# Delta-rule and HGRN2 weights split behind the ended stage's evictions, low parts on VectorE

## The chip, the cores and the metric

One core of a Trainium2 chip. The metric is device time in microseconds. The number shown as before is the median of 3 runs; one further execution was recorded by the hardware profiler, and all rows below are of that execution.

## The reference

One inference step over two layers of a hybrid decoder. Each layer normalizes the stream, multiplies it by one wide input projection, gives groups of columns to four mixers (A = HGRN2, B = gated delta rule, C = Mamba-2 SSD, D = retention), gates their outputs and multiplies them by an output projection. Each mixer reads 2048 prompt tokens, 16 meta tokens ahead of them, and 8 sample tokens that continue stored states.

```python
def layer(h):                       # cut from the reference, in outline
    u = rms_norm(h, w) @ W_in       # columns for A | B (qkv, gate, beta, a) | C (xBC, z, dt) | D
    yA = hgrn2(u_A)                 # vector decay, chunked
    yB = gated_delta(causal_conv(u_B))   # serial over chunks
    yC = ssd(causal_conv(u_C))
    yD = retention(rotary(u_D))
    return h + W_out @ concat(gate * y)
```

## The kernel before

The prompt and the samples lie in 17 tiles: tile 0 with 40 rows (16 meta and 8 sample tokens, padded), and 16 chunks of 128 tokens. Dense work goes over 8 blocks of two tiles (block 0 has three tiles and 296 columns, the others 256). Every layer runs its mixers as stages, in this order: C, B, A, D, output projection. B's dense work comes first in its stage; its serial part, the walk over chunks (`walkB`), is issued in pieces between the work of A and D.

A dense product is made exact enough by splitting both factors into a high and a low part (x = xh + xl, w = wh + wl): three matmuls for each of eight slices of the inner dimension, L484 to L486 in `dense_cm` (weights as the stationary operand, columns of tokens moving), into a tile `pd`; there are two such tiles. A piece of 128 output columns is 24 matmuls for a block; B has eight such pieces (six for q, k, v, which go through a causal convolution, and two for the gate z).

Weights come in pieces of 128 x 1024 numbers (`wpiece`): a transfer into a raw tile `wr` from a pool of five buffers, issued on SP (L451); a cast to the high part `wh` on ScalarE (L458); and a subtraction `wl = wr - wh` (L459), on GpSimd or on VectorE. Which of these two engines it is comes from `lopool`: 1 puts all on GpSimd, 0 all on VectorE, 2 alternates. The stage sets it from the constants PC0, PC1, PB, PA, PD, PO before it calls `weightsB` and so on.

The program is written stage by stage; a scheduler turns it into a queue for each engine, and an engine runs its queue in order. `early()` raises the priority of what is issued under it, so that the scheduler takes it as soon as its inputs are there: the weights of the next stage are split while the stage before still runs. `inorder(names)`, an existing helper, finds the last instruction that has been issued on each named engine, and keeps what is issued under it behind these.

What the names in the rows are: `pd` is a dense product; `u`, `bqk`, `bv` are B's pieces before and after the convolution (L944 to L946 copy them out, L956 and L958 are the taps, L962 and L963 the activation), `cx`, `cb`, `cc` are C's (L954, L958, L962, L963); `z` is a gate (L532, L533). In stage C the chunk work of a tile goes from scores (`tr<-cc,cb`) to a masked product `css` on GpSimd (L1453), a weighted input `cxw` (L1467), the state `SC` (L1479), the output `coi` (L1492 to L1496), a group norm (`fsq`, `fm`, `on`: L606, L612, L616) and a last multiplication on ScalarE into `y` (L1510). The eight samples of tile 0 go through their own steps in between (`decode`) and end with the 40-column `y`, which needs a transfer of the row `dcr` (L1559) first.

Of the kernel before, what the change touches and what calls it, by code (L numbers as in the profile page):

```python
# [93 lines left out]
def body(tc, ctx, a, o, nch, depth, blks, off):  # L94
# [45 lines left out]
    def flush():  # L140
        while pend:
            pend.pop(0)()
# [3 lines left out]
    def hook(n=1):  # L146

        credit[0] += n
        while credit[0] >= 1:
            credit[0] -= 1  # L150
            if walk and next(walk[0], 0) == 0:
                walk.pop()

    @contextmanager
    def inorder(names):

        seen, left = {}, set(names)
        for i in reversed(nc.cur_bb.bb.instructions):
            e = i.engine
            if e in left:  # L160
                seen[e] = i
                left.discard(e)
                if not left:
                    break
        with ExitStack() as st:
            for i in seen.values():
                st.enter_context(tc.issue_after(i))
            yield
# [10 lines left out]
    rA, rB, rD = 1, 1, 1  # L179
    DVEI = ()  # L180
    lopool = [0, 0]
    PC0, PC1, PB, PA, PD, PO = 1, 1, 1, 2, 0, 0
    ACOPY = 1
    WD = 0
    GQ = 1
# [3 lines left out]
    ET = mybir.EngineType  # L189
# [4 lines left out]
    def early():  # L194
        return tc.high_priority(offset=3000)
# [26 lines left out]
    def f4(shape, name, dt=F32):  # L222
        return fp.tile(shape, dt, tag="f4", name=name)
# [38 lines left out]
    def fill():  # L262
        nc.sync.dma_start(cst, a["c_tab"])
        tri = w1([128, 128], "tri")
        nc.sync.dma_start(tri, a["c_retm"][:, 704:832])
        V.tensor_copy(l128r, tri)
        V.tensor_scalar(nbf, C("u32c"), -NEG, NEG, ALU.mult, ALU.add)
        V.tensor_copy(ibf, ident)
        tt(strict, C("u32c"), C("hm0"), ALU.subtract)
        for x in (*sbd, tb, wz, hones):  # L270
            G.memset(x, 0.0)
        G.memset(hones[0:64, 0:1], 1.0)
        G.memset(hones[64:128, 1:2], 1.0)
# [191 lines left out]
    def load_tm(w, cols, wide=False):  # L465
        n = sum(c[1] for c in cols)
        nd = 2 if n == 512 else 4
        r = 128 * nd
        return [wpiece([w[r * k:r * k + r, c0:c0 + cn] for c0, cn in cols], nd, n, wide and k < 2) for k in range(8 // nd)]
# [4 lines left out]
    def load_x(b):  # L474
        b.xh, b.xl = xpair(b.i % 2, BW if b.i % 2 == 0 else 256)
        nc.sync.dma_start(f32(b.xh[:, :, 0:b.n]), f32(xhd[b.i][:, :, :]))
        nc.sync.dma_start(f32(b.xl[:, :, 0:b.n]), f32(xld[b.i][:, :, :]))
# [231 lines left out]
    def weightsA(w):  # L709
        return ([load_cm(w, A_Q + 128 * p) for p in range(2)], [load_cm(w, A_F + 128 * p) for p in range(2)],  # L710
                load_tm(w, [(A_I, 256)]), [load_cm(w, A_Z + 128 * p, True) for p in range(2)])
# [300 lines left out]
    def weightsB(w):  # L1012
        return [load_cm(w, B_QKV + 128 * i) for i in range(6)], [load_cm(w, B_Z + 128 * p, True) for p in range(2)]

    def denseB(L, W, b):

        b.qk, b.v = [blk("bqk") for _ in range(2)], blk("bv")
        qkv = [b.qk[p][:, x] for x in range(2) for p in range(2)] + [b.v[:, p] for p in range(2)]
        conv(L, W[0], b, 0, "B", False, qkv)
        z = blk("z")  # L1020
        for p in range(2):
            dense_cm(W[1][p], b, lambda ps: silu2(ps, z[:, p, 0:b.n], b.n))
            hook(rB)
        nc.sync.dma_start(zdr[b.i], z[:, :, 0:b.n])
        for dst, src in ((slice(0, 4, 2), b.qk[0]), (slice(1, 4, 2), b.qk[1]), (slice(4, 6), b.v)):
            for r in (slice(0, 32), slice(TR0, b.n)) if b.first else (slice(0, b.n),):
                nc.sync.dma_start(qkvd[b.i][:, dst, r], src[:, :, r])
        if b.last:
            conv_out(L, "B", o["gdn_conv_p"][L.l])
# [362 lines left out]
    def weightsC(w):  # L1392
        W = load_tm(w, [(C_Z, 256), (C_Z + 256, 4), (B_AB, 8)], True), []
        for i in range(6):
            if i % 2 == 0:
                yield W
            W[1].append(load_cm(w, C_XBC + 128 * i))
        yield W
# [302 lines left out]
    def prep0(L, b):  # L1701
        b.xh, b.xl = xpair(b.i % 2, BW if b.i % 2 == 0 else 256)
        for t in b.tiles:
            hx = f4([128, D], "hx")
            load_h(0, t, hx)
            xprep(L, t, hx, True)
        for dst, src in ((xhd, b.xh), (xld, b.xl)):
            nc.sync.dma_start(f32(dst[b.i][:, :, :]), f32(src[:, :, 0:b.n]))

    def decode(L, left=False):  # L1710

        while L.dec is not None:
            with inorder(ORD):
                if next(L.dec, 0) == 0:
                    L.dec = None
            if not left:
                return
# [4 lines left out]
    for l in range(depth):  # L1722
        L = Ln
        L.dec = None
        w = a["w_in"][l]
        nextx = (lambda b: prep0(L, b)) if l == 0 else load_x
        if l == 0:
            nextx(blocks[0])
            lopool[0] = PC0
            W = list(weightsC(w))[-1]  # L1730
            fill()
            next(ld)
        else:
            nextx(blocks[0])
        for b in blocks:
            if not b.last:
                nextx(blocks[b.i + 1])
            mixC(L, W, b)
            if not b.first:
                decode(L)  # L1740
        decode(L, True)
        lopool[0] = PB
        with early():
            W = weightsB(w)
        load_x(blocks[0])
        P = None
        walk.append(walkB(L))
        for i in range(-1, nblk, 2):
            bs = blocks[max(i, 0):i + 2]
            for b in bs:  # L1750
                if not b.last:
                    load_x(blocks[b.i + 1])
                denseB(L, W, b)
                if L.dec is not None:
                    decode(L)
            if P is not None:
                L.walkq.append(P)
                if P.first:
                    credit[0] = -WD
            if WEARLY and bs[-1].last:  # L1760
                lopool[0] = PA
                with early():
                    W = weightsA(w)
            with early():
                P = prepB(L, bs)
            if P.first:
                L.dec = decB(L, P.ys, P.epsq)
            decode(L)
        L.walkq.append(P)
        while L.dec is not None:  # L1770
            hook()
            decode(L)
        for x in sq128:
            G.memset(x, 0.0)
        for weights, mix in ((weightsA, mixA), (weightsD, mixD)):
            if not (WEARLY and weights is weightsA):
                lopool[0] = PD
                with early():
                    W = weights(w)
            load_x(blocks[0])  # L1780
            for b in blocks:
                if not b.last:
                    load_x(blocks[b.i + 1])
                mix(L, W, b)
                if not b.first:
                    decode(L)
            flush()
            decode(L, True)
        while walk:
            hook()  # L1790
        lopool[0] = PO
        with early():
            W = [load_tm(a["w_out"][l], [(512 * qd, 512)], qd == 0) for qd in range(2)]
        if l + 1 < depth:
            ld = load_layer(l + 1)
            Ln = next(ld)
            next(ld)
        else:
            Ln = None
            fnw = f4([128, D], "fnw")  # L1800
            nc.sync.dma_start(fnw, a["final_norm_w"].partition_broadcast(128))
        for t in range(NT):
            if t == NT - 1 and Ln is not None:
                lopool[0] = PC1
                parts = weightsC(a["w_in"][l + 1])
                W = outproj(L, W, t, Ln, parts)
            else:
                outproj(L, W, t, Ln)
# [48 lines left out]
```

## Time and profile before

| | |
|---|---|
| median of 3 runs | 2852.36 us (2849.44 to 2856.09) |
| profiled execution, its own time | 2860.07 us |
| its span, first to last instruction | 2858.1 us |
| mean granted TensorE clock | 0.978 of full speed |
| TensorE, matmuls | 2702.7 us, 95% of the span |
| VectorE | 1712.1 us, 60% |
| ScalarE | 1038.7 us, 36% |
| GpSimd | 1066.1 us, 37% |

An engine's busy time is the sum of its instructions in the recorded execution. The profiled execution was 7.7 us longer than the median of the others.

### The profile page before, as it was taken

How to read it: one execution, taken by the hardware profiler on the slowest of the kernel's cores; microseconds unless marked ns; L12 is line 12 of the kernel's file. 1: busy time of each engine (PE TensorE's matmuls, PEld its weight loads, DVE VectorE, ACT ScalarE, POOL GpSimd, SP SyncE). 2: the span in 40 equal slices, each digit the busy share in tenths (PEclk: the TensorE clock that was granted, in tenths of full speed). 3: DMA queues.
4: the chain of work that ended last, by engine and by line, in shares of the span. 5: the costliest groups of instructions: out<-in, count | busy, mean ns of one | idle time of the engine just before them, and what ended most of it. 6: DMA issues, size and time to landing. Idle time of an engine off the chain costs nothing.

```text
span 2858.1 us, 64542 instructions
## 1 busy us (share of the span) xinstructions
PE 2702.7 (95%) x25300; PEld 2461.8 (86%) x25300; DVE 1712.1 (60%) x4872; ACT 1038.7 (36%) x2621; POOL 1066.1 (37%) x2032
## 2 busy tenths in 40 slices
PE   6989999989999899999988999999999999999998
PEld 6889898889889789888878999989888887888887
DVE  5677765657656655464445767756676666445533
ACT  4445532333434422232243445223334443222321
POOL 4453546468323221210032535556673322212100
PEclk9999999999999999999999999999999999999999
DMA  7243455463321423236772423544632223331443
GB/s 177 69 139 106 148 136 146 130 175 103 108 74 61 149 77 113 77 99 212 224 227 80 127 104 115 154 121 140 181 106 72 76 89 109 99 102 67 145 140 111
DMA packets 385143, 349.16 MB, mean 122 GB/s; under 512 B 144312, under 2 KB 349616, under 8 KB 374600
## 3 DMA queue, kind: packets, MB, share of 16 engines
q1 hardware_dynamic: 381320, 335.95, 38.7%
q0 software_dynamic: 3520, 9.09, 1.6%
q8 instruction: 200, 3.28, 0.5%
q14 instruction: 103, 0.84, 0.1%
HBM read 247.05 MB, written 98.10 MB: 121 GB/s over the span
## 4 chain that ended last, share of the span: by engine, by line
PE 76%; DVE 8%; DMA 6%; ACT 3%; POOL 3%; issue 2%; SPq 1%; POOLq 0%; ACTq 0%; DVEq 0%
PE pd L494 10%; PE pd L495 9%; PE pd L497 9%; PE pd L484 9%; PE pd L485 9%; PE pd L486 9%; PE tr L236 7%; PE wo L236 4%; PE sc L236 4%; PE o L236 3%; DMA wr<-in_w_in_dram 3%; PE tr L623 1%; ACT wh L458 1%; PE tr L519 1%; DMA bld<-qkv 1%
## 5 line engine op out<-in xcount | busy, mean ns | idle before, releaser
L484 PE MATMUL pd<-xh,wh 128*128 128x256 f32 (+1 forms) x2816 | 826.9, 294 | 36.9 <-ACT wh L458 11.6
L485 PE MATMUL pd<-xl,wh 128*128 128x256 f32 (+1 forms) x2816 | 817.6, 290 | 0.0
L486 PE MATMUL pd<-xh,wl 128*128 128x256 f32 (+1 forms) x2816 | 813.2, 289 | 1.2 <-DVE wl L459 0.7
L484 PEld LDWEIGHTS pd<-xh,wh 128*128 128x128 f32 x2816 | 542.5, 193 | 58.1 <-issue 15.0
L494 PE MATMUL pd<-wh,xh 128*128 128x512 f32 (+5 forms) x1632 | 563.8, 346 | 8.1 <-DVE sraw L1409 5.1
L495 PE MATMUL pd<-wl,xh 128*128 128x512 f32 (+5 forms) x1632 | 560.0, 343 | 3.8 <-POOL wl L459 3.8
L485 PEld LDWEIGHTS pd<-xl,wh 128*128 128x128 f32 x2816 | 542.1, 193 | 5.5 <-issue 2.7
L486 PEld LDWEIGHTS pd<-xh,wl 128*128 128x128 f32 x2816 | 542.5, 193 | 4.5 <-issue 1.7
L497 PE MATMUL pd<-wh,xl 128*128 128x512 f32 (+4 forms) x1600 | 544.6, 340 | 0.0
L494 PEld LDWEIGHTS pd<-wh,xh 128*128 128x128 f32 (+1 forms) x1632 | 307.1, 188 | 44.8 <-issue 5.5
L495 PEld LDWEIGHTS pd<-wl,xh 128*128 128x128 f32 (+1 forms) x1632 | 307.4, 188 | 38.8 <-POOL wl L459 4.2
L497 PEld LDWEIGHTS pd<-wh,xl 128*128 128x128 f32 (+1 forms) x1600 | 299.8, 187 | 34.7 <-issue 2.0
L313 DVE TENSOR_TENSOR sbd<-low,tr 64x128 f32<-64x128 f32 x384 | 108.9, 284 | 122.0 <-PE tr L236 110.5
L336 POOL TENSOR_TENSOR fm<-fm,expo 128x4 f32<-128x4 f32 (+3 forms) x136 | 133.0, 978 | 85.4 <-DVE fm L614 78.0
L612 POOL TENSOR_SCALAR fm<-fm 128x4 f32<-128x4 f32 (+3 forms) x102 | 22.1, 216 | 363.2 <-DVE fm L609 335.8
L1683 DVE TENSOR_TENSOR hx<-hx,pd 128x512 f32<-128x512 f32 (+1 forms) x72 | 49.5, 687 | 153.1 <-PE pd L497 148.0
L340 POOL TENSOR_SCALAR rm<-rm 128x1 f32<-128x1 f32 (+1 forms) x51 | 14.1, 277 | 337.6 <-ACT junk L358 336.7
L244 POOL COPY bwi<-wz 32x256 f32<-32x256 f32 x128 | 58.7, 458 | 197.9 <-DVE wz L1267 195.6
L1171 POOL TENSOR_TENSOR bR<-bR,bW 128x120 f32<-128x120 f32 (+14 forms) x300 | 118.5, 395 | 20.3
L532 ACT ACTIVATE th<-pd 128x256 f32<-128x256 f32 (+2 forms) x162 | 62.6, 386 | 174.4 <-PE pd L486 130.3
L1170 POOL TENSOR_TENSOR bW<-bU,bR 128x120 f32<-128x120 f32 (+14 forms) x300 | 114.0, 380 | 29.8 <-DMA bR<-bscr 9.5
L458 ACT CAST wh<-wr 128x1024 fp32r<-128x1024 f32 x80 | 83.1, 1044 | 89.1 <-DMA wr<-in_w_in_dram 67.3
(524 smaller groups left out, 5055.7 us busy)
## 6 DMA issues: line engine op xcount, KB each, us to landing
xh<-xh SPq DMA_DIRECT2D x56, 1024.0 KB
xl<-xl SPq DMA_DIRECT2D x56, 1024.0 KB
wr<-in_w_in_dram SPq DMA_DIRECT2D x64, 512.0 KB
hx<-in_x_prompt_dram SPq DMA_DIRECT2D x32, 512.0 KB
y<-y SPq DMA_DIRECT2D x128, 128.0 KB
yf<-y SPq DMA_DIRECT2D x32, 512.0 KB
bld<-qkv SPq DMA_DIRECT2D x32, 384.0 KB
xh<-xh SPq DMA_DIRECT2D x8, 1184.0 KB
```

Source lines behind the costliest of these rows:

```text
L236: T.matmul(out, l, r, start=start, stop=stop, skip_group_check=True)
L313: tt(new[rr, :, hh], low[rr, :, hh], pv, ALU.add)
L336: G.tensor_tensor(dst, src, e.broadcast_to(list(src.shape)), ALU.pow)
L458: S.copy(hv[:, :, c0:c1], r)
L484: T.matmul(ps, hi[:, d], b.xh[:, d, 0:b.n], start=(d == 0), stop=False)
L485: T.matmul(ps, hi[:, d], b.xl[:, d, 0:b.n], start=False, stop=False)
L486: T.matmul(ps, lo[:, d], b.xh[:, d, 0:b.n], start=False, stop=(d == 7))
L494: T.matmul(ps[0:R, 0:n], xh[:, d], hi, start=(d == 0), stop=False)
L495: T.matmul(ps[0:R, 0:n], xh[:, d], lo, start=False, stop=xl is None and d == 7)
L497: T.matmul(ps[0:R, 0:n], xl[:, d], hi, start=False, stop=(d == 7))
L1170: f(wv, bcm(U_[0:2 * nu, j, j + 1:32], 1, m), bcl(R_[0:2 * nu, 0:m, j], 31 - j), ALU.mult)
L1171: f(R_[0:2 * nu, 0:m, j + 1:32], R_[0:2 * nu, 0:m, j + 1:32], wv, ALU.subtract)
```

## The change

Two constants are set to 0, so that the subtractions of B's and of A's weights all go to VectorE (before: B's all on GpSimd, A's alternating). And the two places that issue these weights stand under `inorder` for ScalarE and VectorE, so that the casts and subtractions come behind the last instruction that was issued there on each of the two engines. The weights of C, D and of the output are not touched.

```diff
-    PC0, PC1, PB, PA, PD, PO = 1, 1, 1, 2, 0, 0
+    PC0, PC1, PB, PA, PD, PO = 1, 1, 0, 0, 0, 0
...
         decode(L, True)
         lopool[0] = PB
-        with early():
+        with early(), inorder((ET.Activation, ET.DVE)):
             W = weightsB(w)
...
             if WEARLY and bs[-1].last:
                 lopool[0] = PA
-                with early():
+                with early(), inorder((ET.Activation, ET.DVE)):
                     W = weightsA(w)
```

How the queues change. On ScalarE, at the end of stage C in layer 0, the queue before has the casts of B's weights between C's last evictions (`cx`, `cb`, `cc`):

```order
L458 CAST wh<-wr 128x1024
L954 ACTIVATE cb<-pd,cbh,cwh 128x256
L962 ACTIVATE th<-cb 128x256
L458 CAST wh<-wr 128x1024 x2
L954 ACTIVATE cc<-pd,cbh,cwh 128x256
L977 COPY cso<-tr 3x384
L458 CAST wh<-wr 128x1024
L954 ACTIVATE cc<-pd,cbh,cwh 128x256
```

The queue of the changed kernel on ScalarE at the same place in the program, from C's last outputs on, down to the first copy of B's first piece:

```order
L1510 ACTIVATE y<-tr,pv 128x128 x2
L606 ACTIVATE fsq,fm<-coi 40x128 x2
L989 COPY cxt<-tr 128x3x24 x2
L1510 ACTIVATE y<-tr,pv 128x40 x2
L458 CAST wh<-wr 128x1024 x7
L944 COPY u<-pd 128x32
L945 COPY usB<-pd 128x8
L946 COPY u<-pd 128x256
L956 ACTIVATE bqk<-u,cwh 128x32
L458 CAST wh<-wr 128x1024
```

The casts have moved behind the output of the sample tile, and seven of the eight stand in a row ahead of the first copy of B's dense product.

On TensorE, before, the matmuls of B's block 0 (128x296) come directly behind C's last dense matmuls (128x256) and a few small ones:

```order
L485 MATMUL pd<-xl,wh 128x256
L486 MATMUL pd<-xh,wl 128x256
L976 MATMUL tr<-ident,hC 3x128
L236 MATMUL tr<-g,cst 128x8
L236 MATMUL tr<-g,l128r 128x8
L236 MATMUL tr<-g,cst 128x8 x2
L976 MATMUL tr<-ident,hC 3x128
L484 MATMUL pd<-xh,wh 128x296
L485 MATMUL pd<-xl,wh 128x296
```

In the changed kernel TensorE's queue has, ahead of B's block 0 in layer 0, the whole chunk work of C's last tiles and the transposes of its outputs (these rows are the end of it):

```order
L236 MATMUL wo<-cxb,css 128x64 x4
L236 MATMUL wo<-SC,cc 128x128 x2
L236 MATMUL tr<-cxw,cxb 128x128 x2
L623 MATMUL tr<-ident,on 128x128 x4
L623 MATMUL tr<-ident,on 128x40
L986 MATMUL tr<-ident,cx 128x96 x2
L623 MATMUL tr<-ident,on 128x40
L484 MATMUL pd<-xh,wh 128x296
L485 MATMUL pd<-xl,wh 128x296
L484 MATMUL pd<-xh,wh 128x296
L485 MATMUL pd<-xl,wh 128x296
L486 MATMUL pd<-xh,wl 128x296
```

B's dense matmuls have moved behind all of these, with no dense matmul between them any more.

On VectorE, at the end of B's dense work in layer 0, the queue before has a subtraction for A's weights between the taps of B's last convolution piece:

```order
L1267 TENSOR_TENSOR wz<-bwi,wo 32x256
L958 SCALAR_TENSOR_TENSOR bv<-pd,cwh,bv 128x256 x2
L459 TENSOR_TENSOR wl<-wr,wh 128x1024
L958 SCALAR_TENSOR_TENSOR bv<-pd,cwh,bv 128x256
L960 COPY hB<-pd 128x3
```

In the changed kernel, the same place on VectorE:

```order
L958 SCALAR_TENSOR_TENSOR bv<-pd,cwh,bv 128x256 x3
L960 COPY hB<-pd 128x3
L385 TENSOR_SCALAR cwh<-cwt 128x48
L963 SCALAR_TENSOR_TENSOR bv<-th,bv 128x256
L645 SCALAR_TENSOR_TENSOR y<-tr,pvh,bz 128x128 x2
L533 SCALAR_TENSOR_TENSOR z<-th,pd 128x256
L1267 TENSOR_TENSOR wz<-bwi,wo 32x256
L313 TENSOR_TENSOR sbd_112<-low,tr 64x2x64
L533 SCALAR_TENSOR_TENSOR z<-th,pd 128x256
L313 TENSOR_TENSOR sbd_112<-low,tr 64x2x64
L1267 TENSOR_TENSOR wz<-bwi,wo 32x256
L459 TENSOR_TENSOR wl<-wr,wh 128x1024 x2
```

The three taps, the closing step and both gate pieces of B's last block have moved ahead of the first subtraction for A; ScalarE's queue shows the same for its part.

## Rows read from the trace of the kernel before

**Rows 1.** The page: span; busy time, share of the span, instructions of TensorE.

```profile
span 2858.1 us, 64542 instructions
...
PE 2702.7 (95%) x25300; PEld 2461.8 (86%) x25300; DVE 1712.1 (60%) x4872; ACT 1038.7 (36%) x2621; POOL 1066.1 (37%) x2032
```

**Rows 2.** Tile wl, all subtractions by engine: min/median/max ns, first and last start.

```profile
L459 POOL TENSOR_TENSOR wl<-wr,wh x40: 2338/2412/2796, 13.2 to 2038.0; 128x1024 fp32r<-128x1024 f32 x40
L459 DVE TENSOR_TENSOR wl<-wr,wh x40: 1200/1224/1505, 607.7 to 2659.2; 128x1024 fp32r<-128x1024 f32 x40
```

**Rows 3.** Timeline of ScalarE, layer 0: start, us, engine, line, operation, out<-in, shapes.

```profile
304.25 1.03 ACT L458 CAST wh<-wr 128x1024 fp32r<-128x1024 f32 x1
...
372.85 0.49 ACT L1510 ACTIVATE y<-tr,pv 128x40 f32<-128x40 f32 x2
```

**Rows 4.** Timeline of TensorE, layer 0, C to B; brackets: idle before, releaser.

```profile
327.15 0.28 PE L486 MATMUL pd<-xh,wl 128*128 128x256 f32 x1
...
336.29 0.46 PE L236 MATMUL tr<-cc,cb 128*128 128x128 f32 x2 [4.50 <-DVE cc L963]
...
341.12 0.39 PE L236 MATMUL tr<-cc,cb 128*128 128x128 f32 x2
...
347.20 0.66 PE L236 MATMUL tr<-cxw,cxb 128*128 128x128 f32 x4
...
356.67 0.66 PE L236 MATMUL tr<-cxw,cxb 128*128 128x128 f32 x4
...
368.54 0.30 PE L486 MATMUL pd<-xh,wl 128*128 128x296 f32 x1
...
371.65 0.25 PE L623 MATMUL tr<-ident,on 40*128 40x40 f32 x1
```

**Rows 5.** Timeline of TensorE, layer 1, C to B.

```profile
1740.60 0.28 PE L486 MATMUL pd<-xh,wl 128*128 128x256 f32 x1
...
1777.64 0.30 PE L486 MATMUL pd<-xh,wl 128*128 128x296 f32 x1
```

**Rows 6.** Timeline of VectorE, layer 0, C to B.

```profile
327.11 0.48 DVE L958 SCALAR_TENSOR_TENSOR cc<-pd,cwh,cc 128x256 f32<-128x256 f32 x1
...
328.10 2.59 DVE L616 TENSOR_TENSOR on<-coi,fm 128x256 f32<-128x256 f32 x1
...
337.54 0.42 DVE L963 SCALAR_TENSOR_TENSOR cc<-th,cc 128x256 f32<-128x256 f32 x1 [0.41 <-ACT th L962]
...
364.41 0.41 DVE L1559 TENSOR_TENSOR dcr<-dcr,dcs 8x256 f32<-8x256 f32 x1
...
367.39 0.41 DVE L1563 TENSOR_TENSOR coi<-o,cz 40x256 f32<-40x256 f32 x1
...
369.60 0.42 DVE L616 TENSOR_TENSOR on<-coi,fm 40x256 f32<-40x256 f32 x1 [1.43 <-POOL fm L336]
```

**Rows 7.** Timeline of GpSimd, layer 0, C to B.

```profile
343.77 0.61 POOL L1467 TENSOR_TENSOR cxw<-cxb,eg 128x256 f32<-128x256 f32 x1 [0.64 <-DVE cxb L1462]
...
353.65 0.61 POOL L1467 TENSOR_TENSOR cxw<-cxb,eg 128x256 f32<-128x256 f32 x1
```

**Rows 8.** Windows: length, busy PE, PEld, DVE, ACT, POOL; clock, DMA share, GB/s.

```profile
337.90:373.40 35.50, 35.50 (x266) 34.55 (x266) 26.18 (x85) 16.99 (x71) 10.27 (x17) 0.97 0.25 70
```

**Rows 9.** Timelines of TensorE and of ScalarE, layer 0, B to A.

```profile
609.55 0.55 PE L484 MATMUL pd<-xh,wh 128*128 128x256 f32 x1 [9.94 <-ACT wh L458]
...
606.65 1.04 ACT L458 CAST wh<-wr 128x1024 fp32r<-128x1024 f32 x1 [10.29 <-DMA wr<-in_w_in_dram]
```

**Rows 10.** Windows, columns as in rows 8.

```profile
609.50:614.30 4.80, 4.75 (x26) 4.78 (x27) 4.74 (x8) 2.21 (x5) 4.53 (x6) 0.60 0.53 141
835.20:845.40 10.20, 7.66 (x33) 6.92 (x34) 5.22 (x16) 2.38 (x7) 3.42 (x7) 0.50 0.06 17
```

**Rows 11.** Window of tile pd alone: PE, PEld, DVE, ACT; clock, DMA, GB/s.

```profile
358.50:366.30 7.80, 7.80 (x58) 7.80 (x58) 0.00 (x0) 1.04 (x6) 1.00 0.28 77
```

**Rows 12.** Timeline of TensorE, layer 1, B to A.

```profile
2010.17 0.40 PE L484 MATMUL pd<-xh,wh 128*128 128x296 f32 x1 [1.62 <-ACT wh L458]
```

## The prediction

> **What bounds the kernel.** I read the page first. TensorE is busy for 2702.7 of 2858.1 us, so some 155 us of the span lie between its matmuls [rows 1]. A kernel like this gains only where TensorE waits, and loses wherever a wait is added that no other matmul fills. So I looked at the stages the change touches: the two places (one per layer) where stage C hands over to B, and the two where B hands over to A.
>
> At C to B, layer 0, the eight casts of B's weights start on ScalarE at 304.25, while C's last dense is still running, and their low parts run on GpSimd [rows 2, 3]. C's last dense matmul ends at 327.15 + 0.28 = 327.43 (call that moment T), B's dense (tile pd, 128x296) is already in the queue behind it, and the last of block 0's 192 dense matmuls ends at 368.54 + 0.30 = 368.84 [rows 4]. In those 41.4 us TensorE has finished both block 0 and nearly all of C's tail: the chunk arithmetic of C's last block and its decode, ending with the 128x40 output on ScalarE at 372.85 + 0.49 = 373.34 [rows 3]. In layer 1 the same stretch goes from 1740.88 to 1777.94, 37.1 us [rows 5]. Layer 0 is longer, partly by the 4.50 us that TensorE waits at 336.29 for C's last convolution result [rows 4].
>
> At B to A, layer 0, TensorE stands still for 9.94 us before 609.55, waiting for a cast of A's first weights; that cast waited for its transfer (10.29 us idle on ScalarE) [rows 9]. The granted clock is 0.60 in the following 4.8 us [rows 10].
>
> **The change part by part.**
>
> 1. *B's weights behind stage C.* The order shows all of C's ScalarE and VectorE work, down to the 128x40 output, ahead of the first cast and subtraction. Behind the waiting cast stand seven casts and then B's evictions; TensorE's queue has only C's tail ahead of B's first dense matmul. So what ran side by side in 41.4 us now runs one after the other, counted from T:
>
> - *C's last convolution piece.* Before, its result is ready at 337.54 + 0.42 = 337.96 [rows 6], 10.5 us behind T, because VectorE was held by operations that took 2.4 to 2.6 us beside GpSimd's subtractions (one at 328.10, 2.59 us [rows 6]). Free of them it is three taps of 0.48, two steps of 0.42, a copy of about 0.5 and hops: I take 3.2 us.
> - *C's tail without filler.* Before: 373.34 − 337.96 = 35.4 us. From it I take the places where C's work was ready and TensorE's queue had B's dense ahead of it. The first score product starts at 341.12, 2.8 us later than it could (0.3 us after 337.96); the state products start at 347.20 and 356.67, though the weighted input on GpSimd was done at 343.77 + 0.61 = 344.38 and at 353.65 + 0.61 = 354.26 (2.8 and 2.4 us); the final transposes start at 371.65, though the row was done at 369.60 + 0.42 = 370.02 (1.6 us) [rows 4, 6, 7]. 35.4 − 9.6 = 25.8 us. The bounds: above, 35.4 us (nothing is won). Below, a sum of work alone: GpSimd's 10.27 us in this stretch [rows 8], ten VectorE steps of 0.42 on the path and one round trip of 2.6 us (367.39 − 364.82, the transfer of the decode row [rows 6]): 17.1 us, with ScalarE's and TensorE's steps taken as nothing. I take 25.8, since it is read from starts and ends in the same stretch.
> - *First cast and hops*: 1.03 [rows 3] + 0.5 = 1.5 us. The first low part, 1.22 us on VectorE [rows 2], lies beside the first matmuls.
> - *192 matmuls of block 0*: 58 of them took 7.80 us where nothing stood between them [rows 11]; 192 × 7.80 / 58 = 25.8; with the first one's length, 26.2 us.
> - *Clock*: I charge what the restart at B to A shows: 4.8 us at 0.60 [rows 10], 1.9 us lost.
> - *VectorE in block 0*: eight subtractions of 1.22 = 9.8 us now lie ahead of evictions that I estimate at 19 us (six convolution pieces, each three taps and a closing step over two groups of columns, at 0.2 to 0.48 a step [rows 6], and two gates), 28.7 in all beside 26.2 of TensorE. I take 2 us, with 0 to 4 as bounds.
>
> Sum: 3.2 + 25.8 + 1.5 + 26.2 + 1.9 + 2.0 = 60.6 us. Layer 0 loses 60.6 − 41.4 = 19.2, layer 1 60.6 − 37.1 = 23.5: together 42.7 us. (At the lower bound of the tail 25.3, at the upper 61.9.) Nothing covers it: no dense of another stage stands in TensorE's queue there, and the delta rule's walk has not begun.
>
> What a stretch without dense work does to the clock is seen at 835.20 to 845.40: it is 0.50, the lower level (1.2 GHz), though TensorE is busy for 7.66 of 10.2 us [rows 10]. The Trainium skill, "TensorE: Matmul & The Clock Gate", Part 1, says the same way round that the default state is throttled and activity releases it; by that rule C's thinly filled tail would run its few matmuls at the lower level too, which would make the tail somewhat longer than 25.8. I count none of that.
>
> 2. *A's weights behind B's dense.* Before, ScalarE's first cast (waiting for its transfer) and VectorE's first subtraction stood ahead of B's last evictions, so block 7's two gate pieces (48 matmuls, at most 6.4 us at block 0's pace) and the walk's steps could not run in the 9.94 us. Now they can: about 7.3 us are filled, leaving 2.6, and with that the clock need not fall, 1.9 us: 9.94 + 1.9 − 2.6 = 9.2 us gained in layer 0, bounds 0 (the transfers move with it) and 11.8 (nothing left). Layer 1 waits 1.62 us at its first such place [rows 12] and some 5 more in shorter ones; I take 2.5, bounds 0 and 6.5. Together 11.7, bounds 0 and 18.3. The low parts moved to VectorE (4 of 8 per layer) cost it 4.9 us per layer beside other work.
>
> 3. *GpSimd relieved.* 16 + 8 subtractions leave it, 2.41 us each, and take 1.22 on VectorE [rows 2]. What its subtractions delayed is in the 3.2 us above.
>
> Net: 42.7 − 11.7 = 31 us longer. The profiled execution took 2860.07 (span 2858.1 and 2.0 around it), so the profiled sum is 2891; that execution lies 7.7 above the median of 2852.36, and on the median's scale it is **2883 us**.
>
> **The rivals.** (a) *Faster: the relief outweighs the wait.* If C's tail is short enough without B's evictions between its steps, the 4.50 us and the whole 18.3 us of B to A decide. With 11.7 gained, the losses must be under 5.85 per layer; so the tail must be at most 25.8 − (21.4 − 5.85) = 10.3 us (21.4 is the mean loss above); with all 18.3 gained, 13.6 us. GpSimd's work alone is 10.27 [rows 8] and it is a chain with VectorE steps between. At a tail of 8 us the layers lose 2 × (21.4 − 17.8) = 7.2 and the time is 2841 to 2848. By the row alone, 24 × (2.41 − 1.22) = 28.6 us of engine time are saved; if each of them had stood on the path the time would be 2824 (0.01 of this rival's chance). The Trainium skill, "GPSIMD Engine Reference", § 3.1, puts a two-input elementwise operation at 1.96 times VectorE's time and says that using VectorE for elementwise work stays the rule; the trace agrees on the ratio (2.41 to 1.22), but the rule says nothing about where the operation stands in a queue. (b) *The tail does not shorten* (35.4 us): 2883 + 19 = 2902. (c) *B to A gives nothing*, because A's transfers land no earlier: 2883 + 11.7 = 2895. (d) *No visible change*: the waits are taken from slack elsewhere in the 155 us. Against it: they are in many small pieces, and a stretch with only C's tail in TensorE's queue is time that 95% of busy leaves no room to make good.
>
> **How the numbers follow.** ±0.2% (5.7 us) is about what a measurement here can tell from no change. Forecast 0.60 (2868 to 2894), (b) 0.10, (c) 0.15, (d) 0.08, (a) 0.07. Tail bounds are −17.4 and +19.2 for both layers together, VectorE ±4, B to A −6.6 and +11.7. The range leaves out (a), most of (d), and the two upper ends together: 2860 to 2904. Faster 0.07, same 0.08, slower 0.85.
>
> **What would show it.** After: in TensorE's rows some 30 us in which only C's tail stands between the last 128x256 of C and the first 128x296 of B, waits put down to VectorE, GpSimd and ScalarE's cast, and the clock near 0.5 there, in both layers; C's last convolution result about 3 us behind T instead of 10.5; VectorE's 2.4 us operations gone; the 9.94 us before A's first matmul down to 1 to 4. It would be wrong if B's first 128x296 came within 12 us of T, or if A's casts still waited 10 us with TensorE idle.

## The result and the profile after

The changed kernel takes 2889.06 us (median of 4 runs, 2881.31 to 2899.72) against 2851.36 us of the kernel before on the same chip (4 runs, 2849.44 to 2856.09): 1.0127 times the time before, 95% interval 1.0103 to 1.0151. The forecast was 2883, with a range of 2860 to 2904. Its executions differ with the granted clock: those of 2895 and 2900 us had a mean of 0.967 and 0.965 of full speed, those of 2881 and 2883 us 0.973 and 0.974.

The profiled execution took 2895.19 us, with a span of 2893.5, 35.4 over the span of the profile before. The first rows of its page:

```profile
span 2893.5 us, 64573 instructions
...
PE 2730.1 (94%) x25300; PEld 2480.9 (86%) x25300; DVE 1708.0 (59%) x4896; ACT 1044.4 (36%) x2621; POOL 1008.4 (35%) x2008
```

TensorE has the same 25300 matmuls and is busy 27 us longer than in [rows 1]: the matmuls themselves have become longer. By windows over TensorE, 19 us of it lie where C hands over to B and 8 us in A's first block, both at a lower granted clock, shown below. GpSimd is relieved (1066.1 to 1008.4 us), which by itself bought little (the run with only the engine changed, below).

The hand-over from C to B, layer 0, on TensorE (start, duration, instruction, in brackets the idle time before and what ended it):

```profile
323.35 0.28 PE L486 MATMUL pd<-xh,wl 128*128 128x256 f32 x1
...
340.35 0.41 PE L623 MATMUL tr<-ident,on 128*128 128x128 f32 x2 [1.01 <-DVE on L616]
347.06 0.69 PE L623 MATMUL tr<-ident,on 128*128 128x128 f32 x2 [6.29 <-DVE on L616]
352.03 0.33 PE L623 MATMUL tr<-ident,on 40*128 40x40 f32 x1 [4.28 <-DVE on L616]
...
354.69 0.61 PE L484 MATMUL pd<-xh,wh 128*128 128x296 f32 x1 [1.56 <-ACT wh L458]
...
386.77 0.30 PE L486 MATMUL pd<-xh,wl 128*128 128x296 f32 x1
```

Against [rows 4]: C's last dense matmul ends at 323.63, and B's first one starts 31.1 us later; before, it stood directly behind. In between there are only the small products of C's tail and waits for its norms, 6.29 and 4.28 us long, then the wait for the first cast. The end of block 0 is at 387.07, so the stretch takes 63.4 us where it took 41.4. The other two engines there, VectorE and ScalarE:

```profile
326.70 0.43 DVE L963 SCALAR_TENSOR_TENSOR cc<-th,cc 128x256 f32<-128x256 f32 x1 [0.41 <-ACT th L962]
```

```profile
353.22 0.48 ACT L1510 ACTIVATE y<-tr,pv 128x40 f32<-128x40 f32 x2
353.59 1.99 ACT L458 CAST wh<-wr 128x1024 fp32r<-128x1024 f32 x2
```

C's last convolution result is ready at 327.13, 3.5 us behind its last dense matmul instead of 10.5 [rows 6], and the first cast follows the sample tile's output without a gap. Layer 1 has the same picture, with the first dense matmul of B 31 us behind C's last and the same two waits:

```profile
1748.87 0.28 PE L486 MATMUL pd<-xh,wl 128*128 128x256 f32 x1
...
1772.48 0.69 PE L623 MATMUL tr<-ident,on 128*128 128x128 f32 x2 [4.73 <-DVE on L616]
1777.45 0.32 PE L623 MATMUL tr<-ident,on 40*128 40x40 f32 x1 [4.28 <-DVE on L616]
1780.10 0.61 PE L484 MATMUL pd<-xh,wh 128*128 128x296 f32 x1 [1.56 <-ACT wh L458]
...
1812.33 0.30 PE L486 MATMUL pd<-xh,wl 128*128 128x296 f32 x1
```

Windows of all engines over C's tail and block 0 in layer 0, over the start and the rest of that block, and over C's tail in layer 1 (length, busy time of PE, PEld, DVE, ACT, POOL, granted clock, DMA share, GB/s):

```profile
323.70:354.60 30.90, 13.57 (x71) 10.52 (x69) 10.12 (x30) 9.18 (x33) 9.33 (x17) 0.70 0.26 89
354.60:387.10 32.50, 31.15 (x209) 29.40 (x209) 25.75 (x75) 19.16 (x58) 0.00 (x0) 0.92 0.29 71
354.70:359.00 4.30, 4.21 (x15) 3.85 (x16) 4.30 (x4) 3.72 (x4) 0.00 (x0) 0.50 0.49 88
361.00:387.10 26.10, 24.92 (x185) 23.53 (x183) 19.99 (x70) 14.88 (x53) 0.00 (x0) 1.00 0.19 52
1749.20:1780.10 30.90, 16.79 (x73) 13.37 (x71) 10.05 (x29) 9.07 (x32) 10.55 (x19) 0.56 0.26 88
```

No engine is busy for more than 17 of the 31 us: the tail is a chain that goes from engine to engine. The mean granted clock of the tail is 0.70 and 0.56 of full speed. In layer 0 it fell to 0.50, the lower level (1.2 GHz), between 329 and 330 us; in the 6 us before, TensorE had run only C's small matmuls, with no wait longer than 1.25 us. B's block 0 begins at the lower level (0.50 up to 359, its first matmul takes 0.61 us) and has the full clock from 361 on (its last takes 0.30).

B to A, layer 0, TensorE:

```profile
618.72 0.40 PE L484 MATMUL pd<-xh,wh 128*128 128x296 f32 x1 [0.55 <-ACT wh L458]
...
632.74 0.85 PE L236 MATMUL tr<-wz,bkt 128*128 128x128 f32 x4 [3.92 <-ACT bdc L1108]
635.28 0.61 PE L484 MATMUL pd<-xh,wh 128*128 128x296 f32 x1 [1.69 <-DVE bsk L1046]
```

and ScalarE:

```profile
617.64 1.03 ACT L458 CAST wh<-wr 128x1024 fp32r<-128x1024 f32 x1
...
629.76 1.04 ACT L458 CAST wh<-wr 128x1024 fp32r<-128x1024 f32 x1 [8.50 <-DMA wr<-in_w_in_dram]
```

The 9.94 us of [rows 9] are gone. They had not stood before A's first matmul, as the prediction calls it: the row has the shape 128x256 and is B's last gate piece, and A's first matmul (128x296) came 4.9 us later in the kernel before:

```profile
614.49 0.38 PE L484 MATMUL pd<-xh,wh 128*128 128x296 f32 x1
```

In the changed kernel the cast of A's fourth piece waits 8.50 us for its transfer, and TensorE idles 3.92 and 1.69 us inside A's block 0. In both layers the granted clock of that block is lower than before (from B's last dense matmul to the end of A's block 0; first the changed kernel, layers 0 and 1, then the kernel before; columns as above):

```profile
615.10:663.80 48.70, 40.19 (x305) 37.70 (x305) 24.60 (x60) 18.59 (x37) 38.08 (x81) 0.89 0.53 156
2038.80:2084.90 46.10, 40.62 (x305) 38.51 (x305) 24.38 (x58) 18.53 (x37) 35.92 (x74) 0.89 0.58 167
```

```profile
614.30:649.60 35.30, 35.30 (x309) 34.20 (x308) 19.43 (x56) 15.81 (x35) 29.02 (x51) 1.00 0.54 171
2007.60:2052.00 44.40, 37.67 (x315) 34.99 (x319) 23.64 (x58) 19.41 (x40) 32.44 (x54) 1.00 0.73 195
```

The queue of SP shows how late the fourth transfer is issued:

```profile
603.30 5.69 SPq L451 DMA_DIRECT2D wr<-in_w_in_dram  x3
...
618.32 0.35 SPq L477 DMA_DIRECT2D xl<-xl  x1
618.78 0.39 SPq L476 DMA_DIRECT2D xh<-xh  x1
...
621.18 12.75 SPq L451 DMA_DIRECT2D wr<-in_w_in_dram  x5
```

Three pieces are issued early; the other five come behind the input of A's second block (two transfers of 1 MB). Before, the fourth piece was issued ahead of that input, and the others between its two halves and behind it. The place on SP's queue is only a small part of the delay, though. The first subtraction for A and the fourth transfer, before:

```profile
607.72 1.22 DVE L459 TENSOR_TENSOR wl<-wr,wh 128x1024 fp32r<-128x1024 f32 x1 [10.27 <-ACT wh L458]
```

```profile
608.97 0.37 SPq L451 DMA_DIRECT2D wr<-in_w_in_dram  x1
```

and the first subtraction in the changed kernel:

```profile
618.70 1.23 DVE L459 TENSOR_TENSOR wl<-wr,wh 128x1024 fp32r<-128x1024 f32 x1 [0.90 <-ACT wh L458]
```

Before, the fourth transfer follows 0.03 us behind the end of the first subtraction (608.94), in the changed kernel 1.25 us behind it (619.93). In both layers of all fourteen profiles of this study the fourth transfer is never issued before the first subtraction has ended, the fifth never before the second, and so on to the eighth; in more than half of these cases it follows 0.03 us later. A subtraction is the last reader of a raw tile. So what the transfers wait for is a free raw tile: the pool of five also holds tiles of B's walk (`bU` at L1159, `bld` at L1187), and going by the three early transfers, three are left for A's weights there. The order moves the end of the first subtraction from 5.4 us ahead of the end of B's last dense matmul to 4.9 us behind it, and the fourth transfer goes with it.

### The profile page after: what moved, and what is told of

Same layout as the page of the kernel before. It is cut to its first block, busy times and chain, and to the rows that moved or that the text cites. A ratio compares the mean times of both kernels' runs of the same rounds, so it can differ in the third digit from the quotient of the medians.

```text
span 2893.5 us, 64573 instructions
## 1 busy us (share of the span) xinstructions
PE 2730.1 (94%) x25300; PEld 2480.9 (86%) x25300; DVE 1708.0 (59%) x4896; ACT 1044.4 (36%) x2621; POOL 1008.4 (35%) x2008
## 5 line engine op out<-in xcount | busy, mean ns | idle before, releaser
L306 ACT ACTIVATE low<-sbd,bEG 128x128 f32<-128x128 f32 x256 | 88.5, 394 | 72.2 <-DVE sbd L313 71.2
```

Source lines behind the costliest of these rows:

```text
L306: S.mul(low[:, p], old[:, p], decay(p))
```

## The experiments

The theory at this point: what costs is the place of B's casts behind C's tail; the engine of the low parts and A's part matter little. The rival: VectorE's extra subtractions cost it. Each run's ratio to the kernel before stands with its 95% interval; the kernel before had 19 to 31 executions beside these runs, with medians of 2855 to 2857 us.

**Only B's part.**

```diff
-    PC0, PC1, PB, PA, PD, PO = 1, 1, 1, 2, 0, 0
+    PC0, PC1, PB, PA, PD, PO = 1, 1, 0, 2, 0, 0
...
-        with early():
+        with early(), inorder((ET.Activation, ET.DVE)):
             W = weightsB(w)
```

> Only B's part: its low parts on VectorE and its split behind stage C; A's weights as before. Theory (the order behind C's tail costs the time, and A's part gives some back): the whole loss and no gain, some 43 us over before, 2885 to 2902; TensorE's waits in C's tail as in the changed kernel, 25 to 31 us from C's last dense matmul to B's first, and the 9.94 us before A's first matmul still there. Rival (A's part does not give anything, or costs): 2889 or under, like the changed kernel.

Measured: 2886.69 us, 1.0097 times before (1.0072 to 1.0122). B's part alone makes nearly the whole loss. The time lies in the range of the theory and in that of the rival too, so it does not say whether A's part gives something back; 43 us over before were expected and the medians differ by 30. Its stretch from C's last dense matmul to the end of block 0 is 64.6 and 63.4 us. The wait of 9.94 us did not stay as it was, against expectation: in layer 0 TensorE waits 5.87 us before transposes of the walk and 1.63 us before B's last gate piece.

**Only A's part.**

```diff
+    PC0, PC1, PB, PA, PD, PO = 1, 1, 1, 0, 0, 0
...
+                with early(), inorder((ET.Activation, ET.DVE)):
                     W = weightsA(w)
```

> Only A's part: its low parts on VectorE and its split behind B's last evictions; B's weights as before. Theory: the 9.94 us before A's first matmul go, part of it comes back as waits for A's fourth to eighth piece, which are fetched later: 2838 to 2851. Rival (the waits only move): 2851 to 2860.

Measured: 2853.01 us, 0.9984 (0.9966 to 1.0002): not to be told from no change, or a gain of up to 0.3%, and in the rival's range. In its profile the 9.94 us are gone and A's block 0 is longer (from B's last dense matmul to its end 48.1 us instead of 35.4 in layer 0), with 7.91 us of ScalarE's wait for the fourth piece: the waits moved.

**Only the engine of the low parts.**

```diff
-    PC0, PC1, PB, PA, PD, PO = 1, 1, 1, 2, 0, 0
+    PC0, PC1, PB, PA, PD, PO = 1, 1, 0, 0, 0, 0
```

> The low parts of B and A on VectorE, nothing about the order: the casts and subtractions start as early as in before. Theory: no loss at C to B, and C's last convolution result comes earlier because VectorE is not beside GpSimd's subtractions: 2838 to 2853. Rival (VectorE's extra work is what costs): 2870 or more.

Measured: 2854.39 us, 0.9982 (0.9968 to 0.9997), at most a small gain and just above the expected range. VectorE's extra subtractions do not cost the loss. The row of `on` shows what they replace; groups by line and shape on VectorE, 300 to 355 us, first of this kernel, then of the kernel before:

```profile
L616 DVE TENSOR_TENSOR on<-coi,fm 128x256 f32<-128x256 f32 x3 | 2.1, 699 | 1.8 <-POOL fm L336 1.8
```

```profile
L616 DVE TENSOR_TENSOR on<-coi,fm 128x256 f32<-128x256 f32 x2 | 5.0, 2490 | 0.0
```

**Only the order.** B's low parts on GpSimd and A's alternating, both under the order.

```diff
+        with early(), inorder((ET.Activation, ET.DVE)):
             W = weightsB(w)
...
+                with early(), inorder((ET.Activation, ET.DVE)):
                     W = weightsA(w)
```

> The order of the changed kernel, with B's low parts on GpSimd and A's alternating as before. Theory: as slow as the changed kernel or somewhat slower, since B's low parts now come one per 2.41 us right where TensorE waits for them: 2885 to 2900. Rival (VectorE's extra work is what costs): 2850 to 2865.

Measured: 2903.51 us, 1.016 (1.0135 to 1.0184), just over the expected range, and the slowest of all, 14 us above the changed kernel in the medians (the two intervals just overlap). The stretch is 73.4 and 72.2 us, 9 to 10 longer than with VectorE; all eight low parts follow one another on GpSimd:

```profile
354.54 18.86 POOL L459 TENSOR_TENSOR wl<-wr,wh 128x1024 fp32r<-128x1024 f32 x8 [3.18 <-ACT wh L458]
```

So the low parts on VectorE are the part of the change that helps, once the order is there.

**B's weights behind C's convolution.** Whether any order costs, or the length of what stands in front: the same `inorder`, issued where the last evictions of C's convolution have been issued, ahead of the chunk work.

```diff
-    PC0, PC1, PB, PA, PD, PO = 1, 1, 1, 2, 0, 0
+    PC0, PC1, PB, PA, PD, PO = 1, 1, 0, 2, 0, 0
...
             conv_out(L, "C", o["ssd_conv_p"][L.l])
+            lopool[0] = PB
+            with early(), inorder((ET.Activation, ET.DVE)):
+                L.WB = weightsB(a["w_in"][L.l])
...
-        lopool[0] = PB
-        with early():
-            W = weightsB(w)
+        W = L.WB
```

> B's low parts on VectorE, and B's weights behind the last evictions of C's convolution on ScalarE and VectorE, ahead of C's chunk tail; A as before. Theory (it is the length of C's tail in front of the casts that costs): B's first dense matmul within 6 us of C's last one, the stretch from C's last dense matmul to the end of B's block 0 at 38 to 45 us, and the time that of before within 0.3%. Rival (any order behind evictions, or VectorE's subtractions, cost the loss): 2875 or more.

Measured: 2842.06 us, 0.9949 (0.9933 to 0.9966): faster than before, where at most 0.3% was expected. The stretch is 41.3 and 40.8 us, as expected; against 41.4 and 37.1 before it has not become shorter, so the gain lies elsewhere (the table below). TensorE at its hand-over, layer 0:

```profile
321.49 0.28 PE L486 MATMUL pd<-xh,wl 128*128 128x256 f32 x1
...
326.29 0.40 PE L484 MATMUL pd<-xh,wh 128*128 128x296 f32 x1
```

B's first dense matmul is 4.5 us behind C's last. From this kernel to the one with only B's part, only the place where B's weights are issued differs; the ratio of the two is 1.0097 / 0.9949 = 1.015, some 42 us, and the two stretches differ by 64.6 + 63.4 − 41.3 − 40.8 = 45.9 us.

**B's weights in the middle of the tail.**

```diff
-    PC0, PC1, PB, PA, PD, PO = 1, 1, 1, 2, 0, 0
+    PC0, PC1, PB, PA, PD, PO = 1, 1, 0, 2, 0, 0
...
         if b.last:
+            lopool[0] = PB
+            with early(), inorder((ET.Activation, ET.DVE)):
+                L.WB = weightsB(a["w_in"][L.l])
             flush()
...
-        lopool[0] = PB
-        with early():
-            W = weightsB(w)
+        W = L.WB
```

> As the kernel with only B's part, but with B's weights issued before the last outputs of C's tail are flushed: on ScalarE the casts stand behind the output of C's last tile but one, ahead of its last tile's and of the sample tile's. Theory (the loss grows with what stands ahead of the casts): B's first dense matmul 17 to 20 us behind C's last instead of 31, the stretch to the end of block 0 at 49 to 53 us, and the time between before and the kernel with only B's part, 2862 to 2876. Rival (VectorE's eight subtractions in block 0 are the cost): as slow as the kernel with only B's part.

Measured: 2851.58 us, 0.9992 (0.9978 to 1.0005). B's first dense matmul comes 20.9 and 20.3 us behind C's last, and the stretch is 54.5 us in both layers, longer than expected, and yet the time is that of before: it was expected 10 us higher at least. The loss in the stretch, 13.1 + 17.4 us, is given back elsewhere: against the averages of the six profiles with B's weights where they were, its profile is some 12 us shorter between B's block 0 and the end of A's block 0 (the table below) and some 15 us from there to the start of stage D (369.8 and 374.1 us in the two layers against 379.3 and 379.9). Why, no run tells; the time does not simply grow with the stretch.

**B behind C's convolution, A behind B's evictions,** all low parts on VectorE: the two edits above together (PB = PA = 0).

> B's weights behind the last evictions of C's convolution, A's behind B's last evictions as in the changed kernel, all low parts of both on VectorE. Theory: none of the loss at C to B and what A's part gives (5 us at most): 2842 to 2856, the fastest so far or level with before. Rival (A's part gives nothing beside B's low parts on VectorE): 2851 to 2862.

Measured: 2844.06 us, 0.9962 (0.995 to 0.9974). Within the expected range, and level with the kernel without A's part: A's part adds nothing beside it, as the rival has it, though that had expected 2851 or more.

**The changed kernel once more.**

> The changed kernel once more, for a second profile: how far the stretches of one kernel differ from one execution to the next. The stretch from C's last dense matmul to the end of B's block 0 should be within 1 us of the first profile (63.4 and 63.5 us) if it is set by the order alone; the others may differ by some us.

Measured: one run of 2880.19 us. The stretch is 64.2 and 62.8 us (63.4 and 63.5 the first time), within the expected 1 us: the order sets it.

**B behind C's convolution, low parts on GpSimd.** As the faster kernel, with PB = 1.

> B's weights behind the last evictions of C's convolution, as in the faster kernel before, but with B's low parts on GpSimd; A as before. Theory (that kernel gains by the engine of the low parts): nothing of the gain is left, since GpSimd works for 19 us on eight low parts where TensorE wants one piece every 3.3 us: 2850 to 2870. Rival (it gains by the place in the queues): 2838 to 2848.

Measured: 2856.68 us, 1.0007 (0.9993 to 1.0022). The stretch is 50.4 and 51.5 us; the gain is gone. Both the place and the engine are needed.

**Only B's low parts on VectorE** (PB = 0, nothing else).

> B's low parts on VectorE and nothing else: casts and subtractions as early as before. Theory (the gain comes from VectorE no longer working beside GpSimd's subtractions): 2836 to 2850, at the level of the kernel with B's weights behind C's convolution. Rival (the place in the queues is needed too): 2850 to 2858.

Measured: 2852.51 us, 0.9994 (0.9979 to 1.0008). The engine alone gives nothing measurable: the theory of this run falls, the rival holds.

**A's first input transferred twice,** on top of only A's part, and, as a control, on the kernel before.

```diff
-    def load_x(b):
+    def load_x(b, times=1):
...
+        for _ in range(times):
             nc.sync.dma_start(f32(b.xh[:, :, 0:b.n]), f32(xhd[b.i][:, :, :]))
             nc.sync.dma_start(f32(b.xl[:, :, 0:b.n]), f32(xld[b.i][:, :, :]))
...
-            load_x(blocks[0])
+            load_x(blocks[0], 2 if weights is weightsA else 1)
```

> The kernel with only A's part, and the two tiles of A's first block's input (1 MB each) are transferred twice, to the same place: 2 MB more in each layer where B hands over to A. Theory (A's part gives nothing because the transfers are the bound there): A's first block ends some 6 us later in each layer, and the time is 5 to 12 us over that of the kernel with only A's part. Rival (the waits for A's fourth piece come from buffers or queue order alone, and the DMA engines have room): within 3 us of it.

> The kernel before, with the same two tiles transferred twice: the control for the run with A's part. Theory (transfers are the bound between B and A whatever the order): 4 to 12 us over before. Rival: within 3 us of before.

Measured: 2850.44 us, 0.9988 (0.9969 to 1.0006), and 2857.41, 1.0011 (0.9997 to 1.0026). Neither moved by more than 3 us, as the rival has it. The rows of SP show that the run missed its place:

```profile
568.27 0.32 SPq L478 DMA_DIRECT2D xl<-xl  x1
568.68 0.73 SPq L477 DMA_DIRECT2D xh<-xh  x1
573.58 0.32 SPq L478 DMA_DIRECT2D xl<-xl  x1
577.06 0.32 SPq L477 DMA_DIRECT2D xh<-xh  x1
...
592.58 7.67 SPq L451 DMA_DIRECT2D wr<-in_w_in_dram  x3
...
607.14 0.53 SPq L478 DMA_DIRECT2D xl<-xl  x1
607.79 0.38 SPq L477 DMA_DIRECT2D xh<-xh  x1
```

A's first input is transferred at 568 to 577, long before its weights; the input that stands ahead of the fourth piece is that of the second block, at 607. So the pair says only that there is room before 590. No run had another place for the second block's input or more raw tiles; that the fourth piece waits for a raw tile rests on the rows above.

**Where the stretches went.** Worked out from TensorE's rows in the fourteen profiles: from C's last dense matmul to the end of B's block 0, and from there to the end of A's block 0, layer 0 / layer 1, in us:

```
                                         C to end of B0   B0 to end of A0
before                                   41.4 / 37.1      280.8 / 274.1
only the engine of the low parts         40.3 / 37.8      275.6 / 282.8
only B's low parts on VectorE            40.6 / 38.6      282.0 / 277.4
only A's part                            42.1 / 37.0      281.4 / 278.5
only A's part, A's input twice           40.8 / 37.0      283.8 / 279.9
before, A's input twice                  40.6 / 37.1      279.4 / 275.3
B behind C's convolution                 41.3 / 40.8      271.1 / 278.1
the same, and A's part                   41.0 / 40.1      273.7 / 275.0
the same without A's part, on GpSimd     50.4 / 51.5      272.8 / 276.2
B in the middle of the tail              54.5 / 54.5      271.2 / 275.0
only B's part                            64.6 / 63.4      271.3 / 272.9
the changed kernel                       63.4 / 63.5      276.8 / 272.3
the changed kernel, second profile       64.2 / 62.8      278.8 / 273.1
only the order                           73.4 / 72.2      272.7 / 274.6
```

The six profiles with B's weights where they were average 280.5 and 278.0 in the second column, the eight with B's weights in any order 273.5 and 274.6: some 10 us over both layers come back there, with A's part or without. (Over both layers the first six lie at 554.7 us or more, the eight at 551.9 or less.) In the profile of the kernel with B behind C's convolution, SP issues six of A's eight pieces ahead of the second block's input:

```profile
577.00 4.74 SPq L451 DMA_DIRECT2D wr<-in_w_in_dram  x3
...
590.75 4.76 SPq L451 DMA_DIRECT2D wr<-in_w_in_dram  x3
...
598.42 0.33 SPq L476 DMA_DIRECT2D xh<-xh  x1
598.79 0.43 SPq L477 DMA_DIRECT2D xl<-xl  x1
```

That fits a shorter hand-over to A, but it was seen in the rows only, and the cause of the 10 us stays open; so does a part of some 5 us that the same kernels gain in layer 0 between the end of A's block 0 and stage D.

## Why the prediction was right, and where its steps were not

*C's last convolution piece*: forecast 3.2 us, measured 3.5. *C's tail*: forecast 25.8; from 327.13 to the end of the 128x40 output at 353.22 + 0.48 = 353.70 it took 26.6. *First cast and hops*: forecast 1.5, measured 0.99 to the first matmul. These three were right to a microsecond, 30.5 against 31.1 us, by taking from the tail of before the time that its ready steps stood behind B's dense matmuls. The parts of that 9.6 us did not all come as charged: the first score product and the last transposes won 2.6 and 1.6 us (2.8 and 1.6 charged), but the first state product still starts 2.2 us after its weighted input, behind other products of C; between the two state products 3.3 us were won where 2.4 were charged. The experiments show that the wait behind the tail is the loss: moving the place where B's weights are issued from behind the tail to behind the convolution, and nothing else, takes 1.5% off.

*Block 0*: the terms of 26.2, 1.9 and 2.0 make 30.1; measured 32.4 and 32.5. At a clock of 0.92 over 32.5 us in layer 0 the clock took an estimated 2.6 of them (1.9 forecast). For evictions TensorE stood still 1.2 us there and 2.1 us in layer 1 (2.0 forecast for VectorE), each time for a copy on ScalarE:

```profile
369.06 0.27 PE L1006 MATMUL tr<-ident,usB 128*8 128x128 f32 x1 [1.18 <-ACT usB L945]
```

The other 2 us or so are a term that the sum left out: 14 small matmuls that stand between the 192 (the transposes of `usB` and first score products of B). The two layers lost 22.0 + 26.4 = 48.4 us where 42.7 were forecast.

*A's weights behind B's dense*: the step that failed. I forecast 11.7 us gained by the order of A's casts. The 9.94 us did go, as forecast, though what could fill them was less than counted: only 24 of the 48 matmuls of the gate pieces came after the wait. But the step counted what comes free on ScalarE and VectorE and left out the raw tiles. A's fourth transfer needs a tile that the first subtraction frees; the order moves that subtraction behind B's evictions, the fourth cast waits 8.50 us, and from B's last dense matmul to the end of A's block 0 it takes 48.8 us where it took 35.4 (layer 0). Nor did the clock stay up: what had been 0.60 over 4.8 us is now 0.89 over 48.7. Alone, A's part gives 0.16% with an interval that reaches to nothing, beside B's part nothing that could be measured. The rival that B to A gives nothing was right about this step, also in its reason that A's transfers land no earlier: the fourth lands later. What came in the place of this gain is the 10 us or so that every kernel with B's weights in order gets between block 0 and A, which I had not foreseen. In the profile of the changed kernel 5.8 us came back there and some 7 us in other places, against a loss that was 5.7 us larger. That the sum came near is in this part luck.

*GpSimd relieved*: counted only in the convolution piece, and rightly. The rival by the engine alone, 28.6 us of saved engine time, is refuted: only the low parts moved gives 0.18%, and B's alone 0.06% with an interval that includes none. The Trainium skill, "GPSIMD Engine Reference", § 3.1, that VectorE is the engine for elementwise work, agrees with the runs where the low parts stand in front of TensorE (73 against 63 us of stretch, 2857 against 2842 us), and says nothing of the place in the queue, which here was worth three times as much.

*Clock*: near 0.5 was expected in the tail; the windows show a mean of 0.56 in layer 1 and 0.70 in layer 0. I had counted nothing for the tail's own matmuls; with 26.6 against 25.8 us little was missing.

## What to carry to other kernels

An order that keeps a stage's preparation behind the ended stage is only as good as the point it is tied to: behind the last work that the preparation would really disturb (here the convolution's evictions, and with the low parts on VectorE 0.5% faster than before), not behind the last instruction issued, which hangs at the end of a chain of small steps that leaves TensorE without work. Before such a tie is made, list what stands ahead of the first instruction on each queue and ask which dense work TensorE has left meanwhile. And when casts and subtractions move, ask which buffers they free and what is fetched into these: a wait taken away on ScalarE came back as a late fourth piece.

## What the runs showed of the hardware

The group norm's `on` on VectorE (128x256, L616) took 2.49 us (mean of two) beside GpSimd's subtractions of 128x1024 numbers, and 0.43 to 0.84 us (mean 0.70 of three) with the subtractions on VectorE; two tiny operations (`eg` 128x8, `cbh` 128x6) went from 2.1 to 0.16 and 0.17 us. Not every operation was stretched: the tap at 332.85, which reads the dense product `pd`, took its usual 0.47 us while GpSimd worked on the same row of three subtractions (kernel before):

```profile
327.98 7.29 POOL L459 TENSOR_TENSOR wl<-wr,wh 128x1024 fp32r<-128x1024 f32 x3
```

```profile
332.85 0.47 DVE L958 SCALAR_TENSOR_TENSOR cc<-pd,cwh,cc 128x256 f32<-128x256 f32 x1
```

So work moved to VectorE did not simply add up. With only the engine changed (busy times of its page below) it takes on 24 subtractions of 1.22 us, 29 us in all, and is busy 1715.3 us where it was busy 1712.1: what else it does became some 26 us shorter. Even so the time gained only 0.18% (interval 0.03 to 0.32).

```profile
PE 2699.5 (95%) x25300; PEld 2461.2 (86%) x25300; DVE 1715.3 (60%) x4896; ACT 1040.7 (37%) x2621; POOL 1013.8 (36%) x2008
```
